# Recurrence values turned by VectorE and stored as rows, learned-token values in one product, and weight roundings placed behind a copy

## The chip, the cores and the metric

One NeuronCore of a Trainium2 chip runs the whole program. The metric is device time in microseconds (us) of one execution. The kernel before was timed in three runs.

## What is computed

One layer of a hybrid decoder on 1024 tokens of width 1024, with 16 learned tokens in front (T = 1040 columns). Only the middle of it matters here:

```python
u = rms_norm(h) @ w_in                    # one projection, 3584 columns
# four recurrence heads (HGRN2), head size 128, in chunks of 128 tokens:
S_t = diag(f_t) S_{t-1} + (1 - f_t) i_t^T ;  o_t = S_t^T q_t
# eight heads of stick-breaking attention, head size 64:
w = exp(log_beta + suffix) ;  out = w @ v
h = h + concat[o_hgrn, o_sb] @ w_out
```

The values `i_t` of the recurrence heads and the values `v` of the attention heads, 16 rows of each belonging to the learned tokens, are what the change is about. A feed-forward block stands before this part and another behind it.

## The kernel before, in words

Every large product is made of pairs of rounded parts (fp32r): an operand is split into a high part (a rounding copy on ScalarE, line 241 for the weights of the projection) and a low part (a subtraction on VectorE, line 243), and three matmuls replace one (lines 258 to 260). The projection's result is transposed: 128 features on the partitions, tokens in the free dimension.

The order of TensorE's instructions is written out by hand; those of the other engines and of the DMA queue on SP are placed by a scheduler, each engine in order. The middle part has these stages:

1. **Attention projections** (723 to 838 us): k, v and q columns of four head pairs. `sb_v` turns the values with VectorE's 32x32 transposes (line 1441), splits them and stores them to `vD` as rows, 128 columns each: 64 of the high part and 64 of the low. It does the learned tokens' group last.
2. **Recurrence columns** (from 838 us): sixteen columns, `v f q g` for each head, walked by `hgrn_fill`. The `v` and `f` columns are taken in four pieces (`PIECES`), `q` and `g` in two halves. `use` empties a piece's PSUM bank on ScalarE (line 1144 for `v`, 1150 and 1151 for `f`, 1158 for `q` and `g`) into a tile of the tag `st`, of which there are four buffers, and stores it to DRAM (`hg_v` and so on). The weights of the next column are loaded and split one column ahead.
3. **Braid** (855 to 1141 us): the attention jobs (`sb_jobs`) with the remaining recurrence columns woven in. A job makes scores `z`, ScalarE and VectorE turn them into weights `sig`, TensorE transposes these (`flip`, line 1504) and multiplies them with the values (lines 1579 and 1581). The group of the learned tokens (`wm`) took two products like each other group: the high weights with both halves of the values, then the low weights with the high values.
4. **Recurrence** (`hgrn_attend`, 1152 to 1270 us): each head's tiles are loaded, and the values, which lie transposed in `vT`, are turned by nine TensorE transposes (`flip`; 1 for the learned tokens, 8 for the chunks), copied to `vm` on VectorE and to `vr` on ScalarE (line 1232). Then come the products of a chunk with itself (`lvl`, line 1244, called "own" below), seven levels of decays and products (line 1279, tile `KP`), transposes of the keys (`knp`), the states (`up`) and the outputs (`op`, `onp`). `weave` interleaves the heads with the output projection's products `wo`; its last numbers are the fill's time and the lanes' work, in ns.

Of the kernel before, what the change touches and what calls it, by code (L numbers as in the profile page):

```python
# [11 lines left out]
F32 = mybir.dt.float32  # L12
F32R = mybir.dt.float32r
# [7 lines left out]
P = 128  # L21
# [9 lines left out]
PIECES = [(0, 264), (264, 264), (528, 256), (784, 256)]  # L31
# [18 lines left out]
class Block:  # L50
# [173 lines left out]
    def split_w(self, view, parts=None):  # L224
# [12 lines left out]
        hi = self.wp.tile([P, n], F32R, tag="wh", name="wh", bufs=self.w_bufs)  # L237
        if self.split_on_vector:
            nc.vector.tensor_copy(hi, raw)
        else:  # L240
            self.rounded = nc.scalar.copy(hi, raw)
        lo = self.wp.tile([P, n], F32R, tag="wl", name="wl", bufs=self.w_bufs)
        nc.vector.tensor_sub(lo, raw, hi.bitcast(F32))
        return hi, lo

    def col_tile(self, w, col):
        return self.split_w(
            w[:, col : col + P].rearrange("(k p) f -> p k f", p=P), self.parted.get(col)
        )
# [877 lines left out]
    def hgrn_fill(self, xh, xl, pool, dst):  # L1127
# [8 lines left out]
        def use(kind, h, ps, c0, n):  # L1136
# [6 lines left out]
            if kind == "v":  # L1143
                nc.scalar.copy(t, ps)
                with self.tc.issue_after(self.last_load.ins):
                    nc.sync.dma_start(dst[kind][h, :, s], t)
                return
            elif kind == "f":
                k = staged(n)
                nc.scalar.activation(t, ps, AF.Sigmoid)  # L1150
                nc.scalar.activation(k, ps, AF.Sigmoid, scale=-1.0)  # L1151
# [5 lines left out]
            else:  # L1157
                nc.scalar.activation(t, ps, AF.Sigmoid)
# [9 lines left out]
        def part(i, ci, c0, n, half):  # L1168
            if ci == 0 and half == 0:
                kept["w"] = self.ahead_w.pop(cols[i])  # L1170
                for c in cols[i + 1 : i + (3 if i == 0 else 2)]:
                    if c not in self.ahead_w:
                        self.ahead_w[c] = self.col_tile(self.a["w_in"][0], c)
                kept["round"] = self.rounds[cols[1]]
# [5 lines left out]
            if half == 1:  # L1180
                with self.tc.issue_after(kept["round"]) if i == 0 else ExitStack():
                    use(*plan[i], kept["ps"], c0, n)

# [10 lines left out]
    def hgrn_attend(self, h, pool, src, oH):  # L1194
# [8 lines left out]
        QA, KB, F, vT = (tile_of(x, n) for x, n in (("QA", SEQ), ("KB", SEQ), ("F", SEQ), ("vT", T)))  # L1203
# [5 lines left out]
        vr = tile_of("vr", SEQ).rearrange("p (c d) -> p c d", d=P)  # L1209
# [3 lines left out]
        Ts = tile_of("Ts", SEQ - 8)  # L1213
        vm, kms = (
            pool.tile([META, P], F32, tag=x, name=x, bufs=3) for x in ("vm", "kms")
        )
# [10 lines left out]

        ps = self.flip(vT, [(0, META)])
        nc.vector.tensor_copy(vm, ps[:META, 0, :])
        for q in range(2):  # L1230
            ps = self.flip(vT, [(META + (4 * q + j) * P, P) for j in range(4)])
            nc.scalar.copy(vr[:, 4 * q : 4 * q + 4, :], ps)
        yield 960, 500
# [76 lines left out]
        kn = vT[:, :SEQ].rearrange("p (c d) -> p c d", d=P)  # L1310
# [6 lines left out]
        g = KB  # L1317
        nc.sync.dma_start(g, src["g"][h])
# [6 lines left out]
        for q in range(2):  # L1325
# [5 lines left out]
            for j in js:  # L1331
# [4 lines left out]
                )  # L1336
        yield 1740, 2500, 5000 if last else 2800
# [94 lines left out]
    def sb_v(self, p, vT, mix, vD):  # L1432
# [6 lines left out]
        for c0, nb, m in ((META, 16, 32), (META + 512, 16, 32), (0, 1, META)):  # L1439
# [4 lines left out]
            yield 0, 800  # L1444
# [4 lines left out]
            for b in range(4):  # L1449
                to = vD[p, b // 2, :m, j0 : j0 + nb].rearrange(  # L1450
                    "r j (i b d) -> r (j i) b d", i=2, b=2
                )
                with self.tc.issue_after(self.last_load.ins):
# [4 lines left out]
            yield 0, 1500  # L1458
# [48 lines left out]
    def sb_jobs(self, keys, fetch, pool):  # L1507
# [29 lines left out]
        def job(p, hh, qs, ks, v, b0):  # L1537
# [15 lines left out]
            def meta():  # L1553
                wm.extend(kept["wm"][0])
# [4 lines left out]
                self.sb_parts([t[:META] for t in wm], ps)  # L1559
# [7 lines left out]
            def values(j):  # L1567
# [3 lines left out]
                if j == b0 + 2:  # L1571
                    w = [t.rearrange("p b t -> p (b t)") for t in wm]
                    vj, c = v[:, 0], slice(0, 256)
# [5 lines left out]
                nc.tensor.matmul(o[:, c], vj, w[0], start=j == 0, stop=False,  # L1579
# [827 lines left out]
```

## Time and profile before

| what | value |
|---|---|
| median of three runs | 1964.71 us (1962.61 to 1965.23) |
| profiled execution | 1965.29 us, of it the span of the trace 1963.6 us |
| granted TensorE clock | 1.00 of full speed |
| TensorE busy | 98% of the span |
| VectorE, ScalarE, GpSimd busy | 71%, 43%, 23% |
| DMA, HBM traffic | mean 181 GB/s in the span |

A row of a timeline gives start, duration, engine, line, operation and tiles, and in brackets the idle time ahead of it with what ended it. Matmuls are pipelined, so a matmul's own duration is longer than its step; the step is the difference between two starts. In a table of windows each row is a stretch of the span with the busy time of every engine.

### The profile page before, as it was taken

The page shows a single profiled execution, that of the slowest core. Times are in us where ns is not written, and L with a number is a line of the kernel's source. Part 1 is how long each engine was busy: PE and PEld are TensorE (multiplying, and loading weights), DVE is VectorE, ACT ScalarE, POOL GpSimd, SP SyncE. Part 2 cuts the span into 40 slices and gives each one's busy share as a digit, 9 for nine tenths or more (in the row PEclk, how much of TensorE's full clock was granted, in tenths as well). Part 3 has the DMA queues.
Part 4 walks back from the last instruction along what each step waited for, and adds up shares of the span by engine and source line. Part 5 has one row for each costly group of instructions (what it writes and reads, how often), then busy time and mean ns, then how long its engine had stood idle before and what let it go on. Part 6 is the DMA issues. An engine that isn't in the chain of part 4 may idle for free.

```text
span 1963.6 us, 30437 instructions
## 1 busy us (share of the span) xinstructions
PE 1928.3 (98%) x10704; PEld 1622.0 (83%) x10704; DVE 1391.6 (71%) x2186; ACT 851.7 (43%) x1711; POOL 449.8 (23%) x626
## 2 busy tenths in 40 slices
PE   7999999999999999999999999999999999999999
PEld 6888888888888888888888978887888888888887
DVE  6977777877678665567777766667567777767774
ACT  6523343334444544356666635433132332344443
POOL 3010100001000003133333332210544545430000
PEclk9999999999999999999999999999999999999999
DMA  6356787757965415865454167655544444469473
GB/s 211 93 160 174 245 278 237 235 208 280 372 226 185 136 47 144 194 175 148 126 143 126 57 249 216 171 204 181 195 117 140 126 137 119 134 236 330 146 232 113
DMA packets 381688, 355.56 MB, mean 181 GB/s; under 512 B 129040, under 2 KB 284560, under 8 KB 381536
## 3 DMA queue, kind: packets, MB, share of 16 engines
q1 hardware_dynamic: 359728, 288.98, 48.2%
q0 software_dynamic: 20768, 64.63, 9.5%
q8 instruction: 85, 1.39, 0.3%
q14 instruction: 67, 0.55, 0.1%
q10 hardware_dynamic: 1040, 0.00, 0.0%
HBM read 237.95 MB, written 115.57 MB: 180 GB/s over the span
## 4 chain that ended last, share of the span: by engine, by line
PE 91%; DVE 4%; DMA 2%; ACT 2%; issue 1%; POOL 0%; SPq 0%; ACTq 0%; DVEq 0%; POOLq 0%
PE o L741 21%; PE qb L459 18%; PE qc L459 12%; PE qa L459 12%; PE proj L258 5%; PE proj L260 5%; PE proj L259 5%; PE flip L1504 2%; PE wo L259 1%; PE wo L260 1%; PE wo L258 1%; PE mq L1010 1%; PE oacc L1579 1%; PE oacc L1581 1%; PE z L1649 1%
## 5 line engine op out<-in xcount | busy, mean ns | idle before, releaser
L459 PE MATMUL qb<-T,wh 128*128 128x512 f32 x1056 | 344.5, 390 | 1.3 <-ACT T L318 0.8
L459 PEld LDWEIGHTS qb<-T,wh 128*128 128x128 f32 x1056 | 198.1, 188 | 46.1 <-issue 2.5
L459 PE MATMUL qa<-B,wh 128*128 128x512 f32 x696 | 226.8, 391 | 0.0
L258 PE MATMUL proj<-xh,wh 128*128 128x512 f32 (+2 forms) x640 | 213.4, 333 | 2.4 <-ACT st L1151 1.3
L741 PE MATMUL o<-t,w 128*128 128x512 f32 x924 | 211.8, 390 | 0.5 <-DVE u L552 0.5
L260 PE MATMUL proj<-xl,wh 128*128 128x512 f32 (+2 forms) x640 | 209.8, 328 | 0.8 <-DVE xl L1973 0.8
L259 PE MATMUL proj<-xh,wl 128*128 128x512 f32 (+2 forms) x640 | 209.7, 328 | 0.0
L741 PE MATMUL o<-parts 128*128 128x512 f32 x924 | 209.6, 389 | 0.0
L459 PE MATMUL qb<-T,wl 128*128 128x512 f32 x528 | 205.4, 389 | 0.0
L741 PEld LDWEIGHTS o<-t,w 128*128 128x128 f32 x924 | 172.8, 188 | 37.3 <-issue 0.8
L741 PEld LDWEIGHTS o<-parts 128*128 128x128 f32 x924 | 173.4, 188 | 36.0
L371 DVE TENSOR_TENSOR wl<-s,wh 128x512 fp32r<-128x512 f32 x160 | 165.8, 1036 | 50.8 <-ACT wh L369 49.8
L369 ACT CAST wh<-s 128x512 fp32r<-128x512 f32 x160 | 99.7, 624 | 188.5 <-PE qb L459 142.3
L459 PEld LDWEIGHTS qa<-B,wh 128*128 128x128 f32 x696 | 130.6, 188 | 27.3 <-DVE B L845 0.3
L369 ACT CAST wh<-raw 128x512 fp32r<-128x512 f32 x120 | 74.6, 622 | 147.3 <-PE qc L459 99.0
L459 PE MATMUL qa<-B,wl 128*128 128x512 f32 x348 | 135.4, 389 | 0.0
L258 PEld LDWEIGHTS proj<-xh,wh 128*128 128x128 f32 x640 | 120.6, 188 | 14.5 <-ACT st L1151 2.0
L260 PEld LDWEIGHTS proj<-xl,wh 128*128 128x128 f32 x640 | 120.5, 188 | 12.1 <-DVE xl L1973 1.2
L259 PEld LDWEIGHTS proj<-xh,wl 128*128 128x128 f32 x640 | 120.5, 188 | 9.9
L459 PE MATMUL qc<-T,wh 128*128 128x512 f32 x352 | 117.0, 394 | 0.0
L459 PE MATMUL qc<-B,wh 128*128 128x512 f32 x352 | 115.1, 390 | 2.0 <-DVE u L552 1.2
L459 PEld LDWEIGHTS qb<-T,wl 128*128 128x128 f32 x528 | 99.1, 188 | 20.4
(398 smaller groups left out, 3853.9 us busy)
## 6 DMA issues: line engine op xcount, KB each, us to landing
raw<-in_ffn_w_in_dram SPq DMA_DIRECT2D x176, 256.0 KB, 3.9
raw<-in_ffn_w_out_dram SPq DMA_DIRECT2D x112, 256.0 KB, 4.4
w2in<-both SPq DMA_DIRECT2D x28, 512.0 KB, 3.4
raw<-in_w_in_dram SPq DMA_DIRECT2D x25, 512.0 KB, 5.1
ks<-kD SPq DMA_DIRECT2D x32, 260.0 KB, 4.7
wout<-both SPq DMA_DIRECT2D x16, 512.0 KB, 3.8
wh<-w2in SPq DMA_DIRECT2D x27, 256.0 KB, 3.5
wl<-w2in SPq DMA_DIRECT2D x27, 256.0 KB, 3.6
```

Source lines behind the costliest of these rows:

```text
L258: nc.tensor.matmul(ps, wh[:, s], xs, start=k == 0, stop=False)
L259: nc.tensor.matmul(ps, wl[:, s], xs, start=False, stop=False)
L260: nc.tensor.matmul(ps, wh[:, s], xl[:, k, c0 : c0 + n], start=False, stop=k == nk - 1)
L369: nc.scalar.copy(hi, src)
L371: self.block_lo = nc.vector.tensor_sub(lo, src, hi.bitcast(F32))
L459: nc.tensor.matmul(ps, a[:, k, :], b[:, k, :], start=start and k == 0 and i == 0, stop=k == 3 and i == 2, skip_group_check=True,)
L741: nc.tensor.matmul(banks[bank][m], y[:, m * P : (m + 1) * P], z, start=start and at == 0 and e == 0, stop=q == nq - 1 and e == 2, skip_gro ...
L1010: nc.tensor.matmul(ps[at : at + 32, at_g, :], self.xm[:, 4 * h + k, :], got[i, h][:, k, :], start=h == 0 and kk == 0, stop=h == 1 and kk = ...
L1504: self.nc.tensor.transpose(ps[:m, j, :], src[:, s0 : s0 + m], self.ident)
L1579: nc.tensor.matmul(o[:, c], vj, w[0], start=j == 0, stop=False, skip_group_check=True)
L1581: nc.tensor.matmul(o[:64, c], vj[:, :64], w[1], start=False, stop=end, skip_group_check=True)
L1649: nc.tensor.matmul(z, q, ks[0][:, s0 : s0 + n], start=True, stop=False)
```

## The change

- `use` no longer stores the `v` pieces as they are. VectorE turns each piece in 32x32 blocks (256 columns, and for the first piece the 16 learned tokens apart from a tile of its own), and four DMAs per piece store rows of 128 bytes, so that `hg_v` holds tokens as rows. `PIECES` becomes 272, 256, 256, 256.
- `hgrn_attend` loads `vm` and `vr` straight from these rows. The nine transposes and their copies go, with a step of 960 in the weave's list, and 114850 becomes 111010. `kn` gets a tile of its own, the gates `g` are loaded into `Ts` (after the states) rather than into `KB` (after the key transposes).
- `sb_v` takes the learned tokens' group first and stores its high part a second time, so that one tile `wm` with the high weights in rows 0 to 15 and the low ones in rows 32 to 47 needs one product instead of two, in all 32 jobs.
- The weights of a recurrence column are loaded as before (at the first column one ahead, not two), but their rounding is placed right behind the ScalarE copy that empties a certain piece (`emptied`): the second piece of a `v` or `f` column, the first half of a `q` or `g` column.

```diff
-PIECES = [(0, 264), (264, 264), (528, 256), (784, 256)]
+PIECES = [(0, 272), (272, 256), (528, 256), (784, 256)]
...
+        def split(after=None):
+            hi = self.wp.tile([P, n], F32R, tag="wh", name="wh", bufs=self.w_bufs)
+            with self.tc.issue_after(after) if after else ExitStack():
...
+                    self.rounded = nc.scalar.copy(hi, raw)
...
+            nc.vector.tensor_sub(lo, raw, hi.bitcast(F32))
+            return hi, lo
+
+        return split if hold else split()
...
             if kind == "v":
-                nc.scalar.copy(t, ps)
-                with self.tc.issue_after(self.last_load.ins):
-                    nc.sync.dma_start(dst[kind][h, :, s], t)
+                self.emptied = nc.scalar.copy(t, ps).ins
+                y = staged(n)
+                at = [(n - 256, s.start + n - 256, 8, 32)] + [(0, 0, 1, META)] * (c0 == 0)
+                for x0, to, nb, m in at:
+                    turned = y[:, :256]
+                    if m < 32:
+                        turned = pool.tile([P, 32], F32, tag="st0", name="st0")
+                    nc.vector.transpose(turned, t[:, x0 : x0 + 32 * nb])
+                    for b in range(4):
+                        rows = dst["v"][h, to : to + m * nb, 32 * b : 32 * b + 32]
+                        with self.tc.issue_after(self.last_load.ins):
+                            nc.sync.dma_start(
+                                rows.rearrange("(j r) d -> r j d", r=m),
+                                turned[32 * b : 32 * b + m].rearrange("r (j d) -> r j d", d=32),
+                            )
                 return
...
-                for c in cols[i + 1 : i + (3 if i == 0 else 2)]:
+                for c in cols[i + 1 : i + 2]:
                     if c not in self.ahead_w:
-                        self.ahead_w[c] = self.col_tile(self.a["w_in"][0], c)
+                        self.ahead_w[c] = self.col_tile(self.a["w_in"][0], c, True)
...
+                if ci == (plan[i][0] in "vf") and callable(self.ahead_w.get(following)):
+                    self.ahead_w[following] = self.ahead_w[following](self.emptied)
...
-        for t, x in ((vT, src["v"][h]), (KB, src["k"][h][:, META:]), (QA, src["q"][h]),
+        for t, x in ((KB, src["k"][h][:, META:]), (QA, src["q"][h]),
                      (F, src["f"][h][:, META:]), (KM, src["k"][h][:, :META]),
-                     (FM, src["f"][h][:, :META])):
+                     (FM, src["f"][h][:, :META]), (vm, src["v"][h, :META]),
+                     (vr, src["v"][h, META:].rearrange("(c t) d -> t c d", t=P))):
...
-        ps = self.flip(vT, [(0, META)])
-        nc.vector.tensor_copy(vm, ps[:META, 0, :])
-        for q in range(2):
-            ps = self.flip(vT, [(META + (4 * q + j) * P, P) for j in range(4)])
-            nc.scalar.copy(vr[:, 4 * q : 4 * q + 4, :], ps)
-        yield 960, 500
...
-        g = KB
-        nc.sync.dma_start(g, src["g"][h])
...
+        g = Ts
+        nc.sync.dma_start(g, src["g"][h])
...
-        for c0, nb, m in ((META, 16, 32), (META + 512, 16, 32), (0, 1, META)):
+        for c0, nb, m in ((0, 1, META), (META, 16, 32), (META + 512, 16, 32)):
...
-                self.sb_parts([t[:META] for t in wm], ps)
+                self.sb_parts([wm[0][at : at + META] for at in (0, 32)], ps)
...
-                nc.tensor.matmul(o[:, c], vj, w[0], start=j == 0, stop=False,
+                nc.tensor.matmul(o[:, c], vj, w[0], start=j == 0, stop=end,
                                  skip_group_check=True)
-                nc.tensor.matmul(o[:64, c], vj[:, :64], w[1], start=False, stop=end,
-                                 skip_group_check=True)
-                if end:
+                if not end:
+                    nc.tensor.matmul(o[:64, c], vj[:, :64], w[1], start=False, stop=False,
+                                     skip_group_check=True)
+                else:
                     self.sb_out(p, hh, b0, o, kept, pool, oD)
...
-                        self.weave(first_half_of_o(), lanes, 64 * 650.0 + 4000.0, 114850.0, steady=True)
+                        self.weave(first_half_of_o(), lanes, 64 * 650.0 + 4000.0, 111010.0, steady=True)
```

The change moves instructions. On TensorE, where a braid job multiplies the learned tokens' group (a tile's number stands behind its name), the rows before are:

```order
L1504 MATMUL flip<-ident,sig 128x128 x4
L1579 MATMUL oacc<-wm_7906,v 128x256
L1581 MATMUL oacc<-wm_7907,v 64x256
L1649 MATMUL z<-ks,qs 128x392
L1650 MATMUL z<-ks,qs 128x392
```

And of the change:

```order
L1525 MATMUL flip<-ident,sig 128x128 x4
L1599 MATMUL oacc<-wm_7927,v 128x256
L1670 MATMUL z<-ks,qs 128x392
L1671 MATMUL z<-ks,qs 128x392
```

The second product is gone and nothing else moves there. On TensorE at the start of the recurrence, behind the last products of the projection that are left out here with "...", the rows before are:

```order
L1504 MATMUL flip<-ident,vT 16x128
L1504 MATMUL flip<-ident,vT 128x128 x8
...
L1244 MATMUL lvl<-QA,KB 128x128 x8
L1504 MATMUL flip<-ident,vT 16x128
L1504 MATMUL flip<-ident,vT 128x128 x8
...
L1279 MATMUL lvl<-QA,KP 128x2x64 x4
L1244 MATMUL lvl<-QA,KB 128x128 x8
L1279 MATMUL lvl<-QA,KP 128x2x64 x4
L1504 MATMUL flip<-ident,vT 16x128
L1504 MATMUL flip<-ident,vT 128x128 x8
L1279 MATMUL lvl<-QA,KP 128x2x64 x4
```

And of the change, up to the first `wo`:

```order
L1258 MATMUL lvl<-QA,KB 128x128 x8
...
L1293 MATMUL lvl<-QA,KP 128x2x64 x4
L1258 MATMUL lvl<-QA,KB 128x128 x8
L1293 MATMUL lvl<-QA,KP 128x2x64 x4
...
L1293 MATMUL lvl<-QA,KP 128x2x64 x8
L1258 MATMUL lvl<-QA,KB 128x128 x8
L1293 MATMUL lvl<-QA,KP 128x2x64 x4
L263 MATMUL wo<-oT,wh 128x512
```

Each "..." between two rows is one group of twelve projection products. Three sets of transposes are gone, and the third head's own products now stand ahead of the first `wo`; before, they stood behind the first head's key transposes. On SP at the first head's columns, where the queue before held one store per `v` piece and the weights of the `q` column were loaded long ahead, the rows of the change are:

```order
L1474 DMA vD<-vhl 32x32x32 x4
L1160 DMA hg_v<-st 32x8x32 x4
L1160 DMA hg_v<-st_8323 16x32 x4
L1474 DMA vD<-vhl 32x32x32 x4
L1160 DMA hg_v<-st 32x8x32 x12
L236 DMA raw<-in_w_in_dram 128x8x128
L1173 DMA hg_k<-st 128x272
L1177 DMA hg_f<-st 128x272
```

Twenty stores of the `v` column now stand ahead of the load of the `q` column's weights (`raw`).

More of the change, by code (lines that the diff above doesn't have):

```diff
@@ L222, in quad_group, with split_w @@
         ]
-    def split_w(self, view, parts=None):
+    def split_w(self, view, parts=None, hold=False):
         nc = self.nc
@@ L1157, in use @@
             else:
-                nc.scalar.activation(t, ps, AF.Sigmoid)
+                self.emptied = nc.scalar.activation(t, ps, AF.Sigmoid).ins
                 nc.vector.tensor_mul(t, t, ps)
@@ L1212, in hgrn_attend @@
         attn = [at8[:, 4 * i : 4 * i + 4, :] for i in range(2)]
[L1213 to L1216, printed above, removed]
+        Ts = tile_of("Ts", SEQ)
         ss, sq = tile_of("ss", 8), tile_of("sq", P)
@@ L1452, in sb_v @@
                 )
+                if c0 == 0:
+                    with self.tc.issue_after(self.last_load.ins):
+                        nc.sync.dma_start(
+                            vD[p, b // 2, :m, 1, 32 * (b % 2) : 32 * (b % 2) + 32],
+                            t.bitcast(F32)[32 * b : 32 * b + m, 0, 0],
+                        )
                 with self.tc.issue_after(self.last_load.ins):
@@ L1553, in meta @@
             def meta():
[L1554 removed]
+                wm.append(kept["wm"][0])
                 kept["wm"].reverse()
@@ L1588, in job @@
             return score, turn, value
[L1590 to L1592 removed]
+        kept["wm"] = [fetch.tile([P, 2, P], F32R, name=f"wm{j}") for j in range(2)]
+        for t in kept["wm"]:
             nc.vector.memset(t.bitcast(F32), 0.0)
[L1594 removed]
+        none = kept["wm"][1].bitcast(F32)[64:]
         for p in range(4):
[L1596 to L1597 removed]
+            for a, r0, r1, c0 in ((0, META, 32, 0), (1, META, 32, 0), (1, 0, META, 64),
+                                  (2, 0, 32, 0), (3, 0, 32, 0)):
                 nc.sync.dma_start(
[L1599 removed]
+                    vD[p, :, r0:r1, a, c0:].rearrange("h r c -> r h c"),
+                    none[: r1 - r0, :, c0:],
                 )
```

48 lines of the change are left out of this document (21 added, 27 removed).

## The prediction

> **What bounds the kernel now.** I read the page first, its busy times and the split of the chain that ended last.
>
> ```profile
> PE 1928.3 (98%) x10704; PEld 1622.0 (83%) x10704; DVE 1391.6 (71%) x2186; ACT 851.7 (43%) x1711; POOL 449.8 (23%) x626
> PE 91%; DVE 4%; DMA 2%; ACT 2%; issue 1%; POOL 0%; SPq 0%; ACTq 0%; DVEq 0%; POOLq 0%
> ```
>
> TensorE (PE) is busy for 98% of the span and carries 91% of the chain. A matmul that goes should therefore shorten the run by its step, unless another engine is late at that place. Next come windows of the stages that the change touches: length, then PE, PEld (weight loads), DVE (VectorE), ACT (ScalarE) and POOL, granted clock, DMA share, GB/s.
>
> ```profile
> 855.00:1141.00 286.00, 277.37 (x1964) 246.75 (x1963) 203.62 (x332) 183.72 (x469) 98.25 (x144) 1.00 0.45 127
> 1157.00:1163.30 6.30, 5.62 (x38) 4.83 (x37) 4.06 (x6) 2.45 (x4) 5.20 (x12) 1.00 1.01 385
> 1163.30:1191.20 27.90, 25.82 (x171) 21.45 (x169) 27.74 (x41) 13.67 (x28) 9.23 (x23) 1.00 0.76 237
> 1191.20:1215.00 23.80, 22.09 (x149) 18.63 (x150) 13.00 (x29) 10.40 (x28) 3.21 (x8) 1.00 0.62 177
> ```
>
> In the braid (first row) TensorE is busy 97% of the time and VectorE 71%. From 1163 to 1191 us, the start of the recurrence, it is the other way: VectorE works 27.74 of 27.90 us. Behind that it has 10.8 us to spare in 23.8. The clock is 1.00 throughout, so nothing is corrected for it. Last, what TensorE waits for in these stages (total us, times, longest):
>
> ```profile
> PE flip L1504 <- DVE wu L1628: 3.0, 7, 0.7
> PE proj L258 <- ACT st L1151: 1.3, 1, 1.3
> PE z L1649 <- ACT sig L1656: 1.2, 4, 0.5
> PE oacc L1581 <- DVE wm L1628: 0.3, 1, 0.3
> ```
>
> They are few and short: in the braid TensorE is nearly gapless.
>
> **Term 1, the second product of the learned tokens.** One of the 32 places, and the group of the removed products' weight loads:
>
> ```profile
> 883.74 0.36 PE L1579 MATMUL oacc<-wm,v 128*128 128x256 f32 x1
> 883.95 0.28 PE L1581 MATMUL oacc<-wm,v 128*64 128x256 f32 x1
> 884.06 0.34 PE L1649 MATMUL z<-ks,qs 128*128 128x392 f32 x1
> L1581 PEld LDWEIGHTS oacc<-wm,v x32: 133/138/138, 883.8 to 1140.8; 128*64 128x64 f32 x32
> ```
>
> The product shows 0.28 us, but its successor starts 884.06 - 883.95 = 0.11 after it. The step is at least 0.11, or at most the 0.14 of its weight load; I take 0.12. 32 x 0.12 = 3.8. The only product left must now wait for VectorE's low weights, as the second one did before; the wait above shows 0.3 once, which I keep as lost. **-3.5 us.**
>
> **Term 2, the values' transposes.** The starts of the transposes and of the product behind them, head by head (the 1st, 2nd, 3rd and 4th):
>
> ```profile
> 1152.07 1.30 PE L1504 MATMUL flip<-ident,vT 128*16 128x128 f32 x9
> 1153.13 0.48 PE L258 MATMUL proj<-xh,wh 128*128 128x512 f32 x1
> 1156.01 1.95 PE L1244 MATMUL lvl<-QA,KB 128*128 128x128 f32 x16
> 1157.80 0.71 PE L1504 MATMUL flip<-ident,vT 128*16 128x128 f32 x5
> ...
> 1159.59 0.48 PE L258 MATMUL proj<-xh,wh 128*128 128x512 f32 x1
> ...
> 1166.65 0.71 PE L1504 MATMUL flip<-ident,vT 128*16 128x128 f32 x5
> 1168.04 0.65 PE L1504 MATMUL flip<-ident,vT 128*128 128x128 f32 x4 [0.68 <-ACT vr L1232]
> 1168.55 1.18 PE L1279 MATMUL lvl<-QA,KP 128*128 128x128 f32 x8
> ...
> 1222.98 1.30 PE L1504 MATMUL flip<-ident,vT 128*16 128x128 f32 x9
> 1224.11 1.06 PE L1279 MATMUL lvl<-QA,KP 128*128 128x128 f32 x8
> ```
>
> 1153.13 - 1152.07 = 1.06; 1159.59 - 1157.80 = 1.79; 1168.55 - 1166.65 = 1.90; 1224.11 - 1222.98 = 1.13. The second and third hold a wait of about 0.7 for ScalarE's copy, as the row of 1168.04 shows. **-5.9 us** in all, 4.75 of it before 1191 us.
>
> [...]
>
> **Term 3, what VectorE gives back.** Three of the four sets lie where VectorE sets the pace, and TensorE's gain arrives there only as far as VectorE also finishes earlier. What waits at the end is `kms` (1190.93), in front of the transposes of the keys.
>
> ```profile
> 1157.10 0.69 DVE L1248 TENSOR_TENSOR attn<-lvl,ident 128x512 f32<-128x512 f32 x1 [3.51 <-PE lvl L1244]
> 1158.00 1.23 DVE L1245 TENSOR_TENSOR QA<-QA,F 128x1024 f32<-128x1024 f32 x1 [0.20 <-PE lvl L1244]
> 1190.93 0.27 DVE L1309 COPY kms<-km 16x128 f32<-16x128 f32 x1
> L1229 DVE COPY vm<-flip x4: 269/278/304, 1152.4 to 1223.3; 16x128 f32<-16x128 f32 x4
> ```
>
> For it: three `vm` copies go, 3 x 0.28 = 0.84. The first head's own products stand where its transposes stood, so they start up to 1156.01 - 1152.07 = 3.94 earlier, and VectorE's work on them, which waited 3.51 for them, starts as much earlier. Against it: by the order, the third head's own work now comes ahead of `kms`, two masks of 0.69 and 1.23 for `QA`, 2.6. So `kms` moves by 0.84 + 3.94 - 2.6 = 2.2 at least; where the 6.30 - 4.06 = 2.2 that VectorE stood idle between 1157.0 and 1163.3 is filled as well, by 4.4. Of 4.75, 0.35 to 2.55 is given back; I take the middle, **+1.5**. The bounds are 0 and all 4.75. The fourth set lies where VectorE has time. Behind a set that goes, the next to be late could be `oT` of the output projection:
>
> ```profile
> 1163.99 3.15 DMA oT<-oD
> 1169.47 0.48 PE L258 MATMUL wo<-oT,wh 128*128 128x512 f32 x1
> ```
>
> It lands at 1167.14, 2.33 before the first `wo`. Ahead of that `wo` the third head's transposes (1.90) go and its own products come (1.79, as 1156.01 to 1157.80 shows for the first head): as good as even. Nothing is added.
>
> **Term 4, the turning on VectorE.** No row shows it at this place; the nearest are the same operation on 512 columns:
>
> ```profile
> L1055 DVE STREAM_TRANSPOSE xts<-xrow x16: 700/705/712, 112.8 to 353.6; 128x512 f32<-128x512 f32 x16
> L1441 DVE STREAM_TRANSPOSE vt<-vTs x12: 170/670/711, 733.2 to 829.4; 128x512 f32<-128x512 f32 x8, 128x32 f32<-128x32 f32 x4
> ```
>
> A piece of 256 columns is half of 705, 0.35; the three columns in the braid hold 12, 4.2 us, and 3 x 0.17 for the learned tokens. It lies beside TensorE, and the braid's 82 us of free VectorE time cover it. It costs where a transpose stands ahead of the weights `wu` that a `flip` waits for: those waits are 3.0 over 7 now. Bounds 0 and 4.7; nearer to the first, as nearly all flips find VectorE done: **+0.5**.
>
> **Term 5, roundings and the change of stage.** `PIECES` has the same sum of columns, so the projection's products cost the same. In the braid weights land a column ahead and their rounding has most of a column to be done in, on a ScalarE that is busy 183.72 of 286: 0; with that cover gone, a column would wait for one rounding, the 1.04 of the first row below. At 838 to 873 us the first head's columns run without a braid to hide in:
>
> ```profile
> 853.54 1.04 ACT L241 CAST wh<-raw 128x1024 fp32r<-128x1024 f32 x1
> ...
> 863.51 1.06 ACT L241 CAST wh<-raw 128x1024 fp32r<-128x1024 f32 x1 [2.48 <-DMA raw<-in_w_in_dram]
> ...
> 856.62 0.39 PE L258 MATMUL proj<-xh,wh 128*128 128x256 f32 x1 [1.32 <-ACT st L1151]
> ```
>
> A rounding of 1.04 on ScalarE now precedes the `f` column's activations, and TensorE waited 1.32 for one of these. Placed behind a fixed copy, this rounding may vanish from that place, a gain of up to the 1.3 and the 1.2 of `z` behind it. But twenty stores now stand ahead of the `q` column's weights, and a rounding that waits 2.48 for its load, as at 863.51, now stands ahead of the third `f` piece's activation. Bounds -2.5 and +2.5; value **0**.
>
> **Sum.** -3.5 - 5.9 + 1.5 + 0.5 + 0 = -7.4. The profiled execution took 1965.29 (span 1963.6 and 1.7 around it), which gives 1957.9; the median of the runs, 1964.71, lies 0.6 lower, which gives **1957.3**.
>
> **Rivals.**
>
> *VectorE is the bound.* At the start of the recurrence only VectorE counts, `kms` doesn't move, and the three sets come back as waits in front of key transposes and levels: 4.75 given back, not 1.5, so 1957.3 + 3.25 = **1960.6**. For it: 27.74 busy of 27.90, and 2.6 of new work ahead of `kms`. Against: the work that starts 3.94 earlier.
>
> *The braid isn't TensorE's.* The edit does not do what it says because the freed 3.5 shows up as waits for `sig` and `wu`, and ScalarE and VectorE set the jobs' pace: 1957.3 + 3.5 = **1960.8**. Against: 277.37 busy of 286.
>
> *The waits go too.* No give-back in either stage, and the 2.5 of term 5: 1957.3 - 1.5 - 0.5 - 2.5 = **1952.8**.
>
> *The stores hold up VectorE (slower).* A `v` piece needs four stores with lines of 128 bytes instead of one. The nearest stores of this kind, their issue, and SP's waits in the braid:
>
> ```profile
> L1454 SPq DMA_DIRECT2D vD<-vhl x48: 302/564/2494, 735.4 to 854.5; - x48
> xD<-xts SPq DMA_DIRECT2D x64, 64.0 KB, 3.7
> SPq L1160 <- DVE wu L1628: 35.8, 6, 10.2
> ```
>
> A set takes 4 x 0.56 = 2.3 us to issue and 3.7 to land, 6 us in which it holds one of four `st` buffers. A piece uses two buffers, so the second piece behind it needs the same one. If SP, in order, stands at a wait of up to 10.2 us between copy and stores, the next transpose waits at the head of VectorE's queue; behind it stand the weights `wu`, and the flips wait for these. This decides once SP blocks for more than some 5 us at two pieces of each of three columns: 6 stalls of 2.5 = 15, so **1972**. For it: waits of 10.2. Against: those that were placed around stores today were hidden. [...]
>
> **Chances and range.** Forecast 0.48 (1954 to 1960.7), VectorE the bound 0.20 (1959.5 to 1962), the braid not TensorE's 0.12, the waits go too 0.06, slower 0.14. A measurement tells 0.2% of 1964.71, 3.9 us, from no change: faster is under 1960.8, slower over 1968.6. Half of the VectorE rival counts as faster: 0.48 + 0.06 + 0.10 = 0.64; the other half and the braid rival as the same, 0.22; slower 0.14. The likeliest cases give 1952.5 (the waits go too) to 1964.0 (both of the milder rivals, 1957.3 + 3.25 + 3.5); outside lies mostly the slower case.
>
> **What will show it.** Term 1: the next `z` starts 0.21 behind the learned tokens' product, and no wait for `wm` over 0.5. Term 2: no `flip` from `vT`; the first own products near 1152 less what the braid saved. Term 3: the stretch from the first own products to the end of `kms`, 1191.20 - 1156.01 = 35.2 now, and VectorE's idle time in it. Term 4: waits of `flip` for `wu`, 3.0 now. Term 5: TensorE's waits between 838 and 873. The stores: VectorE's transposes with a wait for `st` stores in brackets. Wrong it would be if those waits exceed 2 us each, or if the recurrence begins earlier and its end doesn't move.

## The result and the profile after

The change makes the kernel slower: 1975.55 us, the median of 5 runs (1974.18 to 1975.99), against 1963.77 of the kernel before in the same comparison. The ratio is 1.0057, with an interval of 1.0044 to 1.0071. The profiled execution took 1974.18 us, of it a span of 1972.5; it is the fastest of the five, so the trace holds 8.9 of the 11.8 us by which the medians differ.

The page's busy times of the kernel after:

```profile
PE 1925.5 (98%) x10636; PEld 1618.9 (82%) x10636; DVE 1400.8 (71%) x2200; ACT 847.0 (43%) x1703; POOL 448.9 (23%) x626
```

TensorE has 68 matmuls less (36 transposes and 32 products) and 2.8 us less busy time, in a span that is 8.9 us longer than before. So the work did go, and TensorE waits more. To see where, four rows are sought that stand in both traces: the first product of the recurrence columns, the first score product of 272 columns in the braid, the last product of a learned tokens' group, and the first product of the recurrence's outputs. Before:

```profile
837.76 0.28 PE L258 MATMUL proj<-xh,wh 128*128 128x264 f32 x1
...
865.48 0.29 PE L1649 MATMUL z<-ks,qs 128*128 128x272 f32 x1
...
1140.79 0.33 PE L1581 MATMUL oacc<-wm,v 128*64 128x256 f32 x1 [0.26 <-DVE wm L1628]
...
1279.54 0.47 PE L258 MATMUL wo<-oH,wh 128*128 128x512 f32 x1
```

And after:

```profile
835.40 0.29 PE L263 MATMUL proj<-xh,wh 128*128 128x272 f32 x1
...
867.73 0.29 PE L1670 MATMUL z<-ks,qs 128*128 128x272 f32 x1
...
1151.42 0.39 PE L1599 MATMUL oacc<-wm,v 128*128 128x256 f32 x1 [0.44 <-DVE wm L1649]
...
1288.35 0.39 PE L263 MATMUL wo<-oH,wh 128*128 128x512 f32 x1
```

The differences of the starts, stage by stage, before and after: up to the columns -2.4; the first columns without a braid 27.7 and 32.3, **+4.6**; the braid 275.3 and 283.7, **+8.4**; the recurrence 138.8 and 136.9, **-1.8**. That sums to the 8.8 by which the last row is late. The -2.4 is taken as scatter: in all the profiled executions below the columns start between 835.1 and 838.9.

**The first columns.** Windows of the kernel after around TensorE's longest wait there (columns as before: PE, PEld, DVE, ACT, POOL, granted clock, DMA, GB/s):

```profile
852.90:856.60 3.70, 0.03 (x1) 0.00 (x0) 1.43 (x3) 2.02 (x4) 0.99 (x5) 0.77 0.99 332
856.60:860.00 3.40, 3.40 (x16) 3.40 (x17) 1.06 (x4) 0.61 (x2) 0.00 (x0) 0.50 0.74 175
860.00:861.80 1.80, 1.80 (x10) 1.80 (x10) 0.00 (x0) 0.79 (x1) 0.00 (x0) 0.52 1.02 336
861.80:864.00 2.20, 2.20 (x21) 2.20 (x20) 1.81 (x3) 0.88 (x3) 0.00 (x0) 1.00 0.97 299
```

TensorE stands still for 3.7 us, where it waited 1.32 before, and behind that the granted clock is 0.50 for 5 us: 26 products take 5.2 us, where behind them 21 take 2.2. The wait costs 2.4 more than before (3.68 - 1.32); that leaves 2.2 of the stage's 4.6 for the half clock. The rows of ScalarE and VectorE say what TensorE waited for:

```profile
854.57 1.28 ACT L1167 ACT_TABLE_LOAD   x1 [2.62 <-DVE st L1156]
```

```profile
853.35 0.77 DVE L1439 SCALAR_TENSOR_TENSOR olo<-kT,kg,ohi 128x528 fp32r<-128x528 f32 x1 [1.54 <-DMA qD<-olo]
854.03 0.44 DVE L1156 STREAM_TRANSPOSE st<-st 128x256 f32<-128x256 f32 x1
```

The first `f` activation waits for VectorE's transpose of the last `v` piece, since a piece now takes two of the four `st` buffers. That transpose stands in order behind a subtraction of the attention's keys, which waits for a transfer of its own.

**The braid.** What TensorE waits for between 870 and 1143 us (total, times, longest), and the longest of these waits:

```profile
PE flip L1525 <- DVE wu L1649: 6.0, 9, 2.2
PE z L1670 <- ACT sig L1677: 3.2, 5, 1.4
PE flip L1579 <- DVE wu L1649: 1.7, 1, 1.7
```

```profile
1082.31 0.30 PE L1525 MATMUL flip<-ident,sig 128*128 128x128 f32 x1 [2.20 <-DVE wu L1649]
```

Just ahead of it on ScalarE and on VectorE:

```profile
1079.04 0.60 ACT L1175 ACTIVATE st<-proj 128x512 f32<-128x512 f32 x1 [1.55 <-PE proj L265]
1079.53 1.04 ACT L244 CAST wh<-raw 128x1024 fp32r<-128x1024 f32 x1
1080.47 0.38 ACT L1648 CAST wu<-flip 128x256 fp32r<-128x256 f32 x1
```

```profile
1080.60 1.22 DVE L246 TENSOR_TENSOR wl<-raw,wh 128x1024 fp32r<-128x1024 f32 x1 [0.25 <-ACT wh L244]
1081.75 0.42 DVE L1649 TENSOR_TENSOR wu<-flip,wu 128x256 fp32r<-128x256 f32 x1
```

The rounding of the next column's weights stands right behind the copy of line 1175, as the change asks, and so ahead of the job's `wu` on ScalarE, and its difference `wl` ahead of `wu` on VectorE. In the kernel before, nothing stands between them at this place, on ScalarE and on VectorE:

```profile
1071.86 0.60 ACT L1158 ACTIVATE st<-proj 128x512 f32<-128x512 f32 x1 [1.57 <-PE proj L260]
1072.35 0.37 ACT L1627 CAST wu<-flip 128x256 fp32r<-128x256 f32 x1
```

```profile
1072.49 0.69 DVE L1159 TENSOR_TENSOR st<-st,proj 128x512 f32<-128x512 f32 x1 [0.94 <-ACT st L1158]
1073.10 0.42 DVE L1628 TENSOR_TENSOR wu<-flip,wu 128x256 fp32r<-128x256 f32 x1
```

`wu`'s low part starts 1.24 behind the start of the copy there, and 2.71 behind it in the kernel after (1079.04 to 1081.75): 1.5 us later. The flip waits 0.61 before and 2.20 after, and the clock falls behind the longer wait, which the windows of the kernel after show:

```profile
1080.20:1083.60 3.40, 1.26 (x8) 0.86 (x8) 3.07 (x5) 2.85 (x9) 0.25 (x1) 1.00 0.34 118
1083.60:1087.00 3.40, 2.83 (x9) 2.47 (x10) 2.02 (x4) 1.05 (x3) 3.32 (x4) 0.50 0.60 191
1087.00:1088.70 1.70, 1.70 (x8) 1.38 (x8) 0.00 (x0) 0.00 (x0) 0.24 (x2) 1.00 0.00 0
```

In the 3.4 us ahead of the half clock TensorE was busy for 1.26. The same order of instructions stands at 989 to 992 (a wait of 1.70, no half clock) and in the last job, where three waits of 0.39, 0.94 and 0.44 come one after the other and a half clock behind them:

```profile
1148.50:1151.80 3.30, 1.53 (x9) 0.93 (x8) 2.55 (x5) 1.78 (x5) 0.32 (x1) 1.00 0.21 79
1151.80:1155.20 3.40, 3.40 (x10) 2.67 (x9) 2.93 (x20) 0.77 (x2) 1.62 (x2) 0.51 0.33 116
```

### The profile page after: what moved, and what is told of

Read it like the earlier page. It is cut to its first block, busy times and chain, and to the rows that moved or that the text cites. A ratio compares the mean times of both kernels' runs of the same rounds, so it can differ in the third digit from the quotient of the medians.

```text
span 1972.5 us, 30442 instructions
## 1 busy us (share of the span) xinstructions
PE 1925.5 (98%) x10636; PEld 1618.9 (82%) x10636; DVE 1400.8 (71%) x2200; ACT 847.0 (43%) x1703; POOL 448.9 (23%) x626
## 5 line engine op out<-in xcount | busy, mean ns | idle before, releaser
L263 PE MATMUL proj<-xh,wh 128*128 128x512 f32 (+3 forms) x640 | 215.5, 337 | 5.0 <-ACT st L1168 3.7
L265 PE MATMUL proj<-xl,wh 128*128 128x512 f32 (+3 forms) x640 | 211.6, 331 | 0.8 <-DVE xl L1995 0.8
L264 PE MATMUL proj<-xh,wl 128*128 128x512 f32 (+3 forms) x640 | 211.8, 331 | 0.0
```

The costliest lines, as they stand in the source:

```text
L263: nc.tensor.matmul(ps, wh[:, s], xs, start=k == 0, stop=False)
L264: nc.tensor.matmul(ps, wl[:, s], xs, start=False, stop=False)
L265: nc.tensor.matmul(ps, wh[:, s], xl[:, k, c0 : c0 + n], start=False, stop=k == nk - 1)
```

## The experiments

All medians are in this table, with the three stages measured in each trace as above (first columns, braid, recurrence). "Before" in the ratio is the kernel before on the same chip, and the rows come from several chips: between them the median of the kernel before moves by 0.9 us, so smaller differences between two rows' medians are not to be read. A stage is read from one execution. Two of these are the slowest of their kernel, before + one product (1967.74) and before + held roundings (1981.23).

| kernel | median us | ratio, interval | columns | braid | recurrence |
|---|---|---|---|---|---|
| before | 1963.6 to 1964.5 | | 27.7 | 275.3 | 138.8 |
| after | 1975.55 | 1.0057, 1.0044 to 1.0071 | 32.3 | 283.7 | 136.9 |
| roundings as before | 1966.18 | 1.0010, 1.0001 to 1.0020 | 32.7 | 275.0 | 136.1 |
| turned values in own buffers | 1980.02 | 1.0076, 1.0063 to 1.0088 | 35.9 | 284.0 | 135.9 |
| both of these | 1964.45 | 1.0000, 0.9991 to 1.0008 | 30.7 | 275.4 | 135.8 |
| before + one product | 1963.59 | 0.9997, 0.9988 to 1.0006 | 31.1 | 273.9 | 140.4 |
| before + held roundings | 1976.07 | 1.0054, 1.0041 to 1.0067 | 30.3 | 286.2 | 140.1 |
| before + rows | 1966.19 | 1.0006, 0.9998 to 1.0015 | 33.2 | 275.2 | 135.5 |
| after, wait filled | 1973.49 | 1.0043, 1.0031 to 1.0055 | 31.1 | 283.8 | 137.5 |
| one buffer per piece | 1962.12 | 0.9988, 0.9979 to 0.9996 | 30.1 | 275.2 | 135.5 |
| one product, GpSimd | 1963.67 | 0.9999, 0.9990 to 1.0008 | 31.5 | 271.7 | 137.0 |
| one buffer, GpSimd | 1960.01 | 0.9979, 0.9970 to 0.9988 | 28.8 | 273.0 | 135.2 |
| one buffer, wait filled | 1960.89 | 0.9985, 0.9977 to 0.9994 | 28.7 | 275.0 | 135.2 |
| one buffer, GpSimd, filled | 1960.59 | 0.9985, 0.9976 to 0.9994 | 32.6 | 272.0 | 135.5 |

**Roundings as before** (in the kernel after):

```diff
-                for c in cols[i + 1 : i + 2]:
+                for c in cols[i + 1 : i + (3 if i == 0 else 2)]:
...
-                        self.ahead_w[c] = self.col_tile(self.a["w_in"][0], c, True)
+                        self.ahead_w[c] = self.col_tile(self.a["w_in"][0], c)
```

> The kernel after, with only the roundings of the recurrence columns' weights undone: they are placed by the scheduler as before, and the first column loads two ahead. Theory 1 (a rounding of 1.04 us on ScalarE and its difference of 1.23 us on VectorE, put right behind a copy, stand ahead of the braid's own roundings wu, and flips and products wait): the waits at 985, 1082 and 1149 to 1152 us and those for sig at 878 and 901 go, with the half clock behind two of them. By the lags at these places 0.9 + 0.9 + 1.6 + 3.0 + 3.8 = 10.2 us less than the kernel after, about 1965. Rival, theory 2 (the turned values hold the staging buffers, and VectorE is late because of the transposes): the braid's waits stay, at most 2 us are gained, 1973.5 or more. Under both, the wait of 3.7 us at 853 to 857 us stays.

Measured: 9.4 us less than the kernel after, and 8.7 less in the braid. The waits of flips for `wu` are short again, with none over 0.7:

```profile
PE flip L1525 <- DVE wu L1649: 4.3, 10, 0.7
```

The wait in the first columns is still there, 4.75. Theory 1 holds, and theory 2 does not explain the braid. VectorE's transposes bear that out: in the braid of the kernel after they wait 0.2 us in all for a store of a staging buffer.

**Held roundings alone** (in the kernel before; the copies that empty a piece are kept, and the roundings placed behind them, as in the change):

```diff
-                        self.ahead_w[c] = self.col_tile(self.a["w_in"][0], c)
+                        self.ahead_w[c] = self.col_tile(self.a["w_in"][0], c, True)
...
+                following = cols[i + 1] if i + 1 < len(plan) else None
+                if ci == (plan[i][0] in "vf") and callable(self.ahead_w.get(following)):
+                    self.ahead_w[following] = self.ahead_w[following](self.emptied)
```

> The kernel before, with only the roundings of the recurrence columns' weights placed behind copies (and loaded one column ahead at the first, too). Theory 1: they alone make the braid wait, so that it loses the 9.4 us that undoing them gave back in the kernel after, about 1974. Rival: they cost only together with the transposes' load on VectorE, and alone less than 3 us, under 1967.5.

Measured: 1976.07, 11.9 us more than the kernel before, and 10.8 more in the braid. This part of the change is by itself as dear as the whole change. It doesn't need the transposes' load. Its six executions lie between 1971.90 and 1981.23. The mean granted clock is 1.000 in the fastest and 0.996 in the slowest, so some 7.7 us are the waits themselves, and the rest goes with how often a half clock follows.

**Turned values in buffers of their own** (in the kernel after):

```diff
-                y = staged(n)
+                y = pool.tile([P, 256], F32, tag="sty", name="sty", bufs=2)
```

> The kernel after, with the turned values in two buffers of their own instead of the four staging buffers. Theory 2 for the stretch from 853 to 857 us: the f column's first activation there waits for a staging buffer that the fourth v piece's transpose on VectorE still reads; with buffers of its own it doesn't, TensorE's wait of 3.7 falls to about 1.3 as in the kernel before, and the half clock behind it goes: 2.4 + 2.3 = 4.7 us less, about 1971. Rival (the activation is held by something else, such as the loading of its table or the store of an earlier piece): the wait stays and the time is that of the kernel after, 1975.5. Under both, the braid's waits stay.

Measured: slower, by 4.5 us. The wait that was aimed at did fall, from 3.7 to 1.09. From the first product of the columns to the end of this wait it is 18.6 us here and with both edits, 18.9 in the kernel before, and 21.2 to 22.3 in three kernels where a `v` piece takes two staging buffers (the kernel after, roundings as before, rows alone). But a longer one took its place behind it, as rows of TensorE and of ScalarE show:

```profile
865.86 0.79 PE L263 MATMUL proj<-xh,wh 128*128 128x512 f32 x1 [5.54 <-ACT st L1168]
```

```profile
864.20 1.04 ACT L244 CAST wh<-raw 128x1024 fp32r<-128x1024 f32 x1 [3.38 <-DMA raw<-in_w_in_dram]
865.15 0.38 ACT L1167 ACTIVATE st<-proj 128x256 f32<-128x256 f32 x1
```

The held rounding stands ahead of the third `f` piece's activation and waits 3.38 for weights whose load was issued at 859.94, behind the stores of the turned values. So the buffer was the cause of the first wait, as expected. The time of the whole came out otherwise, since the held rounding had been hidden behind that wait.

**Both edits together** (in the kernel after):

```diff
+                for c in cols[i + 1 : i + (3 if i == 0 else 2)]:
...
+                        self.ahead_w[c] = self.col_tile(self.a["w_in"][0], c)
...
+                y = pool.tile([P, 256], F32, tag="sty", name="sty", bufs=2)
```

> The kernel after with both edits: roundings placed as before, turned values in two buffers of their own. If the two causes are separate, their gains add: 10.2 + 4.7 = 15 us less than the kernel after, about 1960.5, which is 3 us under the kernel before. If they share a cause, it is no faster than the faster one of them.

Measured: 1964.45. The gains don't add to 15; 11.1 came. The braid is back at 275.4, and three waits of 1.11, 1.23 and 1.54 are left in the first columns, none with a half clock behind it. Against the kernel before, the recurrence is 2.9 shorter and the first columns 3.0 longer, and the one product saves nothing (of that below).

**Rows alone** (in the kernel before: `use`, `hgrn_attend` and the tiles they share, as in the change).

```diff
-PIECES = [(0, 264), (264, 264), (528, 256), (784, 256)]
+PIECES = [(0, 272), (272, 256), (528, 256), (784, 256)]
...
-                nc.scalar.copy(t, ps)
+                self.emptied = nc.scalar.copy(t, ps).ins
+                y = staged(n)
...
+                    nc.vector.transpose(turned, t[:, x0 : x0 + 32 * nb])
```

> The kernel before, with only the values turned by VectorE and stored as rows. The prediction's terms 2 to 4 give -5.9 + 1.5 + 0.5 = -3.9, about 1960.5. Theory 2 (the change of stage pays for it: staging buffers held by the turned values, a stall of 4 to 5 us and half a clock behind it instead of the 1.3 of before): +4.5 on that, about 1965. The gain of the recurrence, from the end of the braid to the first product of the recurrence's outputs with the output weights, is 3.4 to 4.4 under both.

Measured: 1966.19, against 1964.18 of the kernel before in the same comparison; the interval of the ratio still holds 1. The recurrence is 3.2 shorter, a little less than expected, the braid the same (275.2), and the first columns are 5.5 longer, with this wait of TensorE, and a clock of 0.50 for over 5 us behind it:

```profile
858.71 0.58 PE L258 MATMUL proj<-xh,wh 128*128 128x256 f32 x1 [4.23 <-ACT st L1163]
```

Theory 2 holds: the 1960.5 without it lies far outside, and the stage that it names lost 5.5.

**One staging buffer per `v` piece** (in the kernel after with roundings as before):

```diff
-            return pool.tile([P, 512], F32, tag="st", name="st", bufs=4)[:, :n]
+            return pool.tile([P, 528], F32, tag="st", name="st", bufs=4)[:, :n]
...
-            t = staged(n)
+            both = staged(n + 256 * (kind == "v"))
+            t = both[:, :n]
...
-                y = staged(n)
+                y = both[:, n:]
```

> The kernel after, with the roundings placed as before and each v piece and its turned copy in one staging buffer (528 instead of 512 columns wide) instead of two, so that four pieces fill four buffers. Theory 2: the f column's activations no longer wait for buffers of the pieces before, the stall of 4.75 at 853 to 858 us falls to 1.5 and its half clock goes: 4 to 5 us less than 1966.2, about 1961.5. Rival (the stores of 128 bytes land late, whatever holds the buffers): no difference from the kernel with turned buffers of their own, 1964.5.

Measured: 1962.12, 4.1 less than with two buffers a piece, and a little faster than the kernel before (0.9988, 0.9979 to 0.9996). The wait fell from 4.75 to 2.17, not to the expected 1.5. It still costs a half clock: from 857 to 860 the trace shows 0.50.

**The wait filled with products** (in the kernel after, ahead of the third piece of the first `f` column; its products are read by nothing):

```diff
+            if (i, ci, half) == (1, 2, 0):
+                spare = self.pz.tile([P, 512], F32, tag="z", name="spare")
+                for k in range(15):
+                    self.nc.tensor.matmul(
+                        spare, kept["w"][0][:, :P], xh[:, k % KT, :512], start=True, stop=True
+                    )
```

> The kernel after, with 15 products of 512 columns into an unused bank in TensorE's wait at 853 to 857 us, ahead of the third piece of the first f column; nothing reads them. 15 x 0.23 = 3.5 us lie inside the wait of 3.7. Theory 3 (the clock is halved because TensorE stood idle): it stays at 1.00 behind the wait, and the 2.3 us that the half clock cost there are gained, about 1973.3. Rival (the clock falls for another reason, the transfers or the stage): no gain, 1975.5, or a loss where the products outlast the wait.

Measured: 1973.49, 2.1 less. Some executions of the two kernels overlap (1974.18 to 1975.99 and 1970.87 to 1974.48), so the trace has to carry the reading. The idle time that is left is 0.23, and the clock behind it, two windows of this kernel, is full:

```profile
852.79 3.65 PE L1195 MATMUL spare<-xh,wh 128*128 128x512 f32 x15
856.67 0.39 PE L263 MATMUL proj<-xh,wh 128*128 128x256 f32 x1 [0.23 <-ACT st L1168]
```

```profile
856.60:858.00 1.40, 1.33 (x11) 1.33 (x12) 0.78 (x3) 0.30 (x2) 0.00 (x0) 1.00 0.46 92
858.00:860.00 2.00, 1.84 (x17) 1.64 (x15) 0.08 (x1) 0.38 (x1) 0.00 (x0) 1.00 0.67 162
```

The third piece is no earlier at its start (856.67 against 856.60), and yet the column ends 1.8 us earlier: idling had halved the clock (0.50 from 856.60 to 860.00 in the kernel after, 1.00 here). Theory 3 holds. Of the 1.8, 1.2 are left at the end of the stage.

**One product alone** (in the kernel before: `sb_v` and the jobs as in the change):

```diff
-                nc.tensor.matmul(o[:64, c], vj[:, :64], w[1], start=False, stop=end,
-                                 skip_group_check=True)
-                if end:
+                if not end:
+                    nc.tensor.matmul(o[:64, c], vj[:, :64], w[1], start=False, stop=False,
+                                     skip_group_check=True)
+                else:
```

> The kernel before, with only the learned tokens' values done in one product, their group first. If TensorE bounds the braid, as term 1 of the prediction says, 3.5 us less than the kernel before (3.3 to 4.5). Rival (ScalarE and VectorE set the jobs' pace): no difference.

Measured: no difference that can be told (0.9988 to 1.0006; the middle is 0.9 less than the kernel before). The expected 3.5 lies outside. In the trace the braid is 1.4 shorter, and the waits of the flips for `wu` are longer, 4.4 instead of 3.0:

```profile
PE flip L1512 <- DVE wu L1636: 4.4, 9, 0.8
```

With the transposes on VectorE as well, the braid is no shorter at all (275.0 to 275.4 in the kernels with roundings as before). That led to a fourth theory, tried by taking work off VectorE.

The trace shows one thing more. The first columns are 31.1 here against 27.7 before, although no recurrence value is turned in this kernel. TensorE's wait there is 2.00 instead of 1.32, with a half clock from 857 to 860 behind it:

```profile
856.15 0.39 PE L258 MATMUL proj<-xh,wh 128*128 128x256 f32 x1 [2.00 <-ACT st L1151]
```

So a part of what the change lost in the first columns comes with the one product, whose groups `sb_v` stores in another order. Which of its edits makes the wait longer is not shown.

**One product, differences on GpSimd** (in the kernel before with the one product; `low_on_pool` is set while a recurrence column's weights are split):

```diff
-        nc.vector.tensor_sub(lo, raw, hi.bitcast(F32))
+        (nc.gpsimd if self.low_on_pool else nc.vector).tensor_sub(
+            lo, raw, hi.bitcast(F32)
+        )
```

> The kernel before with the one product of the learned tokens, and the differences wl of the recurrence columns' weights on GpSimd instead of VectorE. In the kernel with the one product alone, flips wait 4.4 us for VectorE's wu, against 3.0 before, and the braid is only 1.4 shorter instead of 3.5. Theory 4 (VectorE's queue absorbs what TensorE saves): without 15 differences of 1.2 to 1.5 us VectorE is early, these waits fall under 2.5, and the run takes 2 to 3 us less than with the one product alone, about 1961. Rival (the waits come from the chain of one job, whose length VectorE's other work doesn't change, or GpSimd is too slow with the difference): 1963 or more, no difference.

Measured: the braid is 271.7, 2.2 less than with the one product alone and 3.7 less than before; the flips' waits for `wu` are down to 3.0, not under 2.5. But the time as a whole is 1963.67, as without the edit. The stage does what theory 4 says, and in the trace the first columns give it back: they are 31.5 against 27.7 before, with the same wait of 2.00 as in the kernel with the one product alone, and a half clock behind it. All eleven executions of this kernel have a mean granted clock under 1.000 (0.998 or 0.999), against 8 of 32 of the kernel before. A difference takes 2.4 us on GpSimd:

```profile
L245 POOL TENSOR_TENSOR wl<-raw,wh 128x1024 fp32r<-128x1024 f32 x13 | 31.1, 2396 | 16.8 <-ACT wh L243 16.7
```

**One buffer, differences on GpSimd**, the same edit in the kernel with one staging buffer per piece:

```diff
+        (nc.gpsimd if self.low_on_pool else nc.vector).tensor_sub(
```

> The same move of the differences to GpSimd, in the kernel after with roundings as before and one staging buffer per v piece (1962.1). Theory 4: the transposes took VectorE's time in the braid, and the one product saved nothing there; with VectorE relieved the 3 us come back, about 1959.5. Rival: no difference, 1962.

Measured: 1960.01, 2.1 less, and 2.2 less in the braid. Here stage and median agree. The kernel is faster than the kernel before (0.9979, 0.9970 to 0.9988); against one buffer alone the two intervals still overlap.

**One buffer, wait filled**, with 8 products in place of the 15 above:

```diff
-                for k in range(15):
+                for k in range(8):
```

> The kernel after with roundings as before and one staging buffer per v piece, and 8 products of 512 columns (1.9 us) into an unused bank inside TensorE's wait of 2.2 us at 853.6 to 855.9. Theory 3: a wait of 2.2 still halves the clock for some 4 us, which costs 1.5 to 2; filled, it doesn't, and the run takes about 1960.5. Rival (a wait of 2.2 is too short to matter, or the fill delays the column): no difference or slower, 1962 or more.

Measured: 1960.89, 1.2 less than without them, and 1.4 less in the first columns, with the clock at 1.00. Against the kernel before on the same chip the two ratios are 0.9985 and 0.9988, so the medians alone don't tell these two kernels apart; the stage does what theory 3 says.

**Both in one**, that is in the kernel with one staging buffer per piece:

```diff
+        (nc.gpsimd if self.low_on_pool else nc.vector).tensor_sub(
...
+                for k in range(8):
```

> Both of these together: differences on GpSimd, and the 8 products in the wait. If the two gains are separate they add, about 1958; if GpSimd's part moves the wait to another place, the fill is worth nothing and the time is that of the first.

Measured: 1960.59. They don't add: of the expected 1958 nothing is seen, and the time is that of either alone within the scatter. The first columns are 32.6 in this profile, with a wait of 2.27 behind the filled one: the wait has moved.

## Why the prediction was wrong

It forecast 1957.3, and 1972 for its slower rival. The time was 1975.55, outside the range of 1952.5 to 1964.0. That the slower rival lies near it is luck: it had VectorE's queue held up by stores in the braid, and its transposes wait 0.2 us there.

1. **Term 5 is the step that failed**: "In the braid weights land a column ahead and their rounding has most of a column to be done in ...: 0". They do land early. But a rounding placed behind a copy no longer takes a free moment; it takes the next place in the queue. There it stands ahead of the job's `wu`, with 1.04 us on ScalarE, and its difference with 1.22 on VectorE. Undone, it gives back 9.4; alone, it costs 11.9. The term weighed the cover by how busy ScalarE is, 183.72 of 286, and priced a lost cover at one wait for one rounding. What counts is which instruction is behind it in order, and the term left out the difference on VectorE.
2. **"The clock is 1.00 throughout, so nothing is corrected for it"** held for the profile of before only. The new waits brought it to 0.50, 0.50 and 0.51 in three places: 2.2 us were lost at 856, and up to 1.7 in each of the other two, half of 3.4 us. The last of these, at 1151.8, falls into the recurrence.
3. **The first columns** were given 0 with bounds of 2.5 either way; they cost 4.6. The term named the `q` weights' load behind twenty stores as the danger. That wait exists, but it shows only once the buffers are out of the way (5.54 with buffers of their own). What TensorE waited for first were the `st` buffers, which the slower rival named, but for the braid. There that rival was wrong: rows alone leave the braid at 275.2. The one product adds to this wait as well, 0.7 alone, and term 1 has nothing for it.
4. **Term 1** had the right count and the right size of a product, and the wrong engine. TensorE is busy 97% of the braid, and yet the jobs follow VectorE: the saved 3.5 came to 1.4, with the transposes to nothing, and with VectorE relieved to 3.7. So the rival of the braid that isn't TensorE's was nearer, though not all of the 3.5 was lost with the one product alone.
5. **Term 4** was 0.5, measured -0.1 with rows alone (275.2 against 275.3): free by itself, though a piece takes 0.44 (the row of 854.03) and not 0.35. With the one product it isn't free: the braid's 1.4 are gone.
6. **Terms 2 and 3** together gave -4.4 for the recurrence. Eight kernels with rows and no half clock in this stage take 135.2 to 136.1 us. Of the four with the transposes two have no half clock in it: before with 138.8, and one product with GpSimd, 137.0. That makes about -2.3, between -0.9 and -3.6: right in kind, and half of the size. `kms` starts 45.2 to 45.8 behind the braid's last product in the eight, 49.2 and 50.1 in the two, so its shift of some 4 us lies at the upper end of the 2.2 to 4.4. But about 1.9 of it is lost behind `kms`, where the prediction added nothing. That VectorE would keep all 4.75 was wrong.

## What to carry to other kernels

Before an instruction is pinned to a place in an in-order queue, write down what stands behind it there and who waits for that; ScalarE's queue, idle 36% of the time in the braid before, hid nothing from the instruction right behind (`wu`'s low part started 1.5 us later). A stage whose bounding engine is 97% busy can still be paced by the short waits between its products, as the braid was here (273.9 to 271.7 with the differences off VectorE): take a little work off the other engine to see it. And price TensorE's waits with the half clock that can follow. Several short ones close together (0.39, 0.94 and 0.44 in the last job) brought it here as well as one long one (3.7).

## What the runs showed of the hardware

TensorE's idling halved the granted clock: in the kernel after it was 0.50 from 856.60 to 860.00 behind the wait of 3.7, and with that wait filled 1.00 from 856.60 to 860.00, by products that nothing reads. Ten of the fourteen traces show a half clock between 700 and 1330 us, 18 stretches in all: 15 last 3.4 to 3.6 us (in the kernel after 3.4, from 1083.6 to 1087.0) and three about 7 (with the wait of 3.7, there 6.8 from 854.9 to 861.7, the one of 4.23 and the one of 5.54).

The length of a wait alone doesn't decide. Waits of 2.00, 2.17 and 2.20 were followed by 0.50; one of 2.14 (one buffer, differences on GpSimd) and one of 1.70 (kernel after) were not. The three waits of 0.39, 0.94 and 0.44 in the last job were, and so was this one of 1.27 with held roundings alone (0.21 more of waiting stands behind it), where the trace shows 0.50 from 865.2 to 868.7:

```profile
864.26 0.49 PE L263 MATMUL proj<-xh,wh 128*128 128x512 f32 x1 [1.27 <-ACT st L1156]
```

The work ahead of a half clock tells more. In the kernel after the half clock begins at 854.9, 1083.6 and 1151.85, which is 228.7 and 68.25 apart; 228.7 / 67 and 68.25 / 20 are both 3.41. Cut into stretches of 3.41, each trace by its own starts of a half clock, the ten traces show TensorE busy for at most 1.7 of the 3.41 us ahead of 16 of the 18 starts (in the kernel after for 1.46, 1.26 and 1.65), and for 1.95 ahead of two (both with held roundings alone). At full clock, no stretch with more than 2.0 us of work was followed by a half clock, and several with 1.8 to 2.0 were not either (in the kernel after two, with 1.78 and 1.99). So the work ahead doesn't decide alone either; what does is not shown. For the wait of 2.14 this can't be checked, since its trace has no half clock to place the stretches by.
